# Recurrence operands parked in DRAM, a gate product of 256 columns, and the order of the branch products

## The chip, the cores and the metric

One Trainium2 chip, one of its cores. The kernel is one launch; the metric is the device time of that launch in microseconds. Engines are called by the profile's short names: PE (TensorE, matrix products into PSUM; PEld are its weight loads), DVE (VectorE), ACT (ScalarE), POOL (GpSimd) and SP (SyncE, which here only issues transfers between DRAM and the on-chip memory).

## The reference

Two layers of a hybrid backbone over 512 tokens (256 context, 256 latent) of width 1024. Each layer mixes tokens in two branches and then runs a mixture of 32 experts. What matters here is the mixing:

```
p = h @ w_in                                  # one projection, split by columns
y_rw  = rwkv7_branch(...)                     # 16 heads, recurrence in both directions
y_ssm = ssm_branch(...) * silu(z)             # 32 heads in 8 groups, both directions, gate z
merged = sigmoid(g_rw) * (y_rw @ w_branch_rw) + sigmoid(g_ssm) * (y_ssm @ w_branch_ssm)
out = merged @ w_out
# the recurrence, per head, per token:
sa = S @ a_t
S  = S * w_t + sa b_t^T + v_t k_t^T
y_t = S @ r_t
```

The second layer needs outputs for the latent tokens only, so its branch products, gates and outputs run over 256 tokens instead of 512; its recurrences still pass over all 512.

## The kernel before, in words

Every call of an engine goes through a recorder (`Recorder`, L246 and on), which keeps all calls of a layer, their dependences and their tiles. `finish` gives each call a latest start (`lst`) from the due time of its stream (`rec.at(phase, stream, goal)`), and `schedule` then lists the calls engine by engine: at each step the call that can start first by a table of costs, and among calls that could start at once the one with the earliest `lst`. A tile's slot is part of that: `SLOTS` says how many tiles of a name may live at once, `CLASS` how many slots of a size there are, and a call whose tiles have no slot waits. The emitted order is fixed, and each engine, SP's queue too, takes its instructions in that order. All instructions therefore have one line, L682.

A layer's mixing has three kinds of stream (`mix_streams`): eight pairs of recurrence heads (`rw`), eight state-space groups (`ssm`) with their branch gates (`gate`), and in layer 0 the modulation of the later stages. For a pair, `rw_prep` projects r, k and v (weights come in as `wst`, are split into `wh` and `wl`), and `rw_dir` builds for each direction the products of the chunked recurrence: `Z` (two operands side by side), `XT`, and by `psg` the triangular matrices `QA` and `AR`; `SU` holds the values v by chunk. `rw_solve` inverts the unit triangular matrices on DVE, row by row: `slB` and `slW` are its strip transposes in, 31 pairs of a product `slM` and a reduction into `slY`, and `slO` the transpose out; `rw_merge` (`psW`, `psZ`) completes `TT`. `rw_chain` then forms, per direction, `psat` and `psav`, from them with `TT` `psta` and `psua`, then `psgt` (into `GT`), `psH` and `psra`, and runs the seven steps of state `St` over the chunks, `psH` and `psY`. `rw_out` normalizes (`gy<-psm`), multiplies by the gate (`psgate`) and writes the pair's result to `rwd` in DRAM (`rwo`, `rwq`).

The names r, k, v, Z, XT, AR, QA, SU, TT have as many slots as one pair needs (one, or two for the two directions); `St` uses the slot of `rw_dir`'s `X`, and `GT` that of the solve's `slW`.

`ssm_group` convolves x, B and C on DVE (`cva`), and per 128 tokens computes the gate z: 2 halves of 8 x 3 products of 128 columns (`psz`). Results go to `smd` in DRAM, gates to `gd`.

`merge` loads `rwd` (`rwt`), `smd` (`smt`) and `gd` (`mg`), and for each of eight column blocks j forms the branch products (`psbr`), 24 for R (recurrence) and 48 for S and T (state space), then the gated sum `mhl`; after that the output product `pso`. `route` and `expert`/`expert_rows` follow.

Of the kernel before, what the change touches and what calls it, by code (L numbers as in the profile page):

```python
# [12 lines left out]
F32 = mybir.dt.float32  # L13
# [8 lines left out]
NT = 512  # L22
# [64 lines left out]
def _mix_pieces():  # L87
# [8 lines left out]
    for i in range(8):  # L96
        for n, o in (("x", X_ + 256 * i), ("y", X_ + 256 * i + 128), ("B", B_ + 128 * i), ("C", CC_ + 128 * i),
                     ("z", Z_ + 256 * i), ("u", Z_ + 256 * i + 128)):
            p.append((f"{n}{i}", "in", r(o, 128)))
    for j in range(8):  # L100
        p += [(f"R{j}", "rw", r(128 * j, 128)), (f"S{j}", "ssm0", r(128 * j, 128)), (f"T{j}", "ssm1", r(128 * j, 128))]
# [5 lines left out]
_KDIM = {"in": 8, "rw": 8, "ssm0": 8, "ssm1": 8, "out0": 4, "out1": 4}  # L107
# [20 lines left out]
def pack(i):  # L128
# [7 lines left out]
    src = {"in": f["w_in"], "rw": f["w_branch_rw"], "ssm0": f["w_branch_ssm"][:, :1024],  # L136
# [72 lines left out]
SLOTS = {"R": 2, "sp": 2, "t5": 4, "y5": 3, "rt5": 5, "ot": 2, "z1": 4, "wst": 2, "wh": 2, "wl": 2, "rwst": 1, "rwh": 1, "rwl": 1, "r": 1,  # L209
# [3 lines left out]
CLASS = {"c4": 18, "c2": 40, "c1": 23, "ps": 8}  # L213
# [8 lines left out]
ENGINES = tuple(LAT)  # L222

# [34 lines left out]
class _Pool:  # L258
# [3 lines left out]
    def tile(self, shape, dtype, name=None, tag=None, bufs=None):  # L262
# [6 lines left out]
        if ph == 1:  # L269
            if self.psum and tag == "g":  # L270
                tag = "t"
            if tag in SPLIT and self.rec.stream[0] in ("rw", "sh"):
                tag = "r" + tag
        else:
            tag = f"{tag}.{ph}"
# [410 lines left out]
class Kernel:  # L686
# [10 lines left out]
    def setup(self):  # L697
# [8 lines left out]
        self.unit = t("unit", [128, 512], BF16)  # L706
        self.tri = t("tri", [128, 256], F16)
        self.io = t("io", [128, 256])
        self.iota, self.low = self.io[:, 0:128], self.io[:, 128:256]
# [10 lines left out]
        self.rwd = self.dram.tile([128, 8, 2, NT], F16, name="rwd")  # L720
        self.smd = self.dram.tile([128, 16, 2, NT], F16, name="smd")
# [3 lines left out]
    def constants(self):  # L725
# [4 lines left out]
        u = t([128, 512], F32, "unit32")  # L730
        nc.sync.dma_start(u, i["unit"].rearrange("p j t -> p (j t)"))
        nc.vector.tensor_copy(self.unit, u)
        nc.sync.dma_start(self.io, i["cst"][:, C_WS:C_T64F])
# [322 lines left out]
    def rw_prep(self, l, i):  # L1056
# [23 lines left out]
        vp = rp.tile([128, 64 + NT + 64], F32, name="v", bufs=2)  # L1080
        G.memset(vp[:, 0:64], 0.0)
        G.memset(vp[:, 64 + NT:], 0.0)
        v = S["v"] = vp[:, 64:64 + NT]
# [26 lines left out]
        for w0_ in (0, 4, 8):  # L1110
            pv = self.psum("t", [128, 4, 128], "psv")
            n = min(4, 9 - w0_)
            for w in range(n):
                T.transpose(pv[:, w], vp[:, 64 * (w0_ + w):64 * (w0_ + w) + 128], self.ident)
            if w0_ < 8:
                A.activation(SU[0][64:128, w0_:w0_ + 4, 0], pv[64:128, :, 0:64], AF.Copy)
            a = 0 if w0_ else 1
            A.activation(SU[0][0:64, w0_ + a - 1:w0_ + n - 1, 1], pv[0:64, a:n, 64:128], AF.Copy)
# [118 lines left out]

    def rw_solve(self, i):
# [16 lines left out]
        G.tensor_copy(Y.rearrange("p j t -> p (j t)"), self.unit)  # L1255
# [62 lines left out]
    def rw_chain(self, l, i):  # L1318
# [18 lines left out]
        def batch(name, cs, out, lhs, rhs):  # L1337

            ps = out or self.psum("g", [128, 8, 64], name)
            with nc.together():  # L1340
                for c in cs:
                    for e in E:
                        T.matmul(ps[rows[e], c], lhs(c, e), rhs(c, e), start=True, stop=True)
            return ps

        for d in range(2):
            SU = S["SU"][d]
            TT, XT, Z, AR = [S[x, d] for x in ("TT", "XT", "Z", "AR")]
            qa = S["QA", d].rearrange("p (c e) t -> p c e t", e=2)
            all8 = range(8)  # L1350
            mid = seq[d][1:7]

            ps = batch("psat", all8, None, lambda c, e: Z[rows[e], c, 0], lambda c, e: self.ident[rows[e], 64 * e:64 * e + 64])
            at = wk.tile([128, 8, 64], F32, name="at", tag="slY")
            A.activation(at, ps, AF.Copy)
            ps = batch("psav", all8, None, lambda c, e: qa[rows[1 - e], c, e], lambda c, e: SU[rows[1 - e], c, e])
            av = wk.tile([128, 8, 64], F32, name="av", tag="slB")
            V.tensor_copy(av, ps)
# [4 lines left out]
            ps = batch("psua", all8, None, lambda c, e: TT[rows[e], c], lambda c, e: av[rows[e], c])  # L1363
            A.activation(SU[rows[0], :, 0], ps[rows[0]], AF.Copy)
            V.tensor_copy(SU[rows[1], :, 1], ps[rows[1]])
            ps = batch("psgt", mid, None, lambda c, e: qa[rows[e], c, e], lambda c, e: XT[rows[e], c, 64 * e:64 * e + 64])
# [816 lines left out]
```

## Time and profile before

| | |
|---|---|
| time, median of 3 runs | 3539.37 us (3537.98 to 3549.52) |
| the profiled execution: its time, its span | 3538.96 us, 3537.1 us |
| PE, PEld busy | 3110.2 us (88%), 2094.7 us (59%) |
| DVE busy | 2447.3 us (69%) |
| ACT, POOL busy | 1705.4 us (48%), 769.3 us (22%) |
| bytes moved by DMA | 662.65 MB, 187 GB/s on average |
| granted PE clock, mean | 0.940 of full speed |

Busy times are averages over stages with different limits, so the rows below cut the span: layer 0's mixing until about 1350, its experts until about 2000, layer 1's mixing until about 2990, its experts to the end. In the view by windows a row reads: from:to in us, the length, then busy time (with the count of instructions) of PE, PEld, DVE, ACT and POOL, the mean granted PE clock, the mean busy share of the 16 DMA engines, and GB/s. The clock has two levels, 1.2 and 2.4 GHz; a mean between 0.5 and 1 tells how much of the stretch was at either. In a timeline or a chain of waits a row begins with its start and its length in us; "[... <-X]" is idle time before it and who ended it.

### The profile page before, as it was taken

What the parts mean: (1) busy time and instruction counts of PE and PEld (TensorE: products, weight loads), DVE (VectorE), ACT (ScalarE), POOL (GpSimd) and SP (SyncE); (2) the same over time, 40 slices, a digit from 0 to 9 for tenths busy, and PEclk for the clock granted to TensorE, in tenths of its full rate; (3) what the DMA queues carried; (4) which work ended last, traced back from release to release, by engine and by line L of the source; (5) the groups of instructions that cost most, each with busy time, mean ns of one, the idle gap of its engine ahead of it and who ended that gap; (6) DMA issues with size and microseconds to landing.
All of it is one profiled execution on the core that took longest, in us unless ns stands there. A gap on an engine that the chain in (4) does not pass through costs nothing. (4 is left out here: it accounts for less than half of the span.)

```text
span 3537.1 us, 86322 instructions
## 1 busy us (share of the span) xinstructions
PE 3110.2 (88%) x36050; PEld 2094.7 (59%) x36050; DVE 2447.3 (69%) x4491; ACT 1705.4 (48%) x3155; POOL 769.3 (22%) x1080
## 2 busy tenths in 40 slices
PE   7899889898998998999998778888889789899987
PEld 3566466475566457888886455666566668333332
DVE  4868868768778337999997788788988765221112
ACT  4554454454544325998886645554545434111111
POOL 1332332333232111111111133232333311000000
PEclk9999999999999997999999899999999889899998
DMA  7032231421312736999996411221212138999996
GB/s 283 28 106 73 93 118 51 151 100 43 120 57 98 276 104 222 412 401 397 396 394 249 154 63 45 74 69 50 75 61 71 53 125 299 346 399 398 399 398 243
DMA packets 241746, 662.65 MB, mean 187 GB/s; under 512 B 26688, under 2 KB 55104, under 8 KB 241344
## 3 DMA queue, kind: packets, MB, share of 16 engines
q1 hardware_dynamic: 236608, 640.22, 49.1%
q10 hardware_dynamic: 3584, 12.58, 0.9%
q8 instruction: 287, 4.70, 0.5%
q0 software_dynamic: 1152, 4.19, 0.3%
q14 instruction: 115, 0.94, 0.1%
HBM read 622.30 MB, written 34.60 MB: 186 GB/s over the span
## 5 line engine op out<-in xcount | busy, mean ns | idle before, releaser
L682 PE MATMUL mm<-h,wh 128*128 128x512 f16 (+1 forms) x2432 | 680.4, 363 | 11.0 <-ACT wh L682 11.0
L682 PEld LDWEIGHTS <-wh 128*128 128x128 f16 x3200 | 311.4, 99 | 280.7 <-issue 25.4
L682 PE MATMUL mm<-h,wl 128*128 128x512 f16 (+2 forms) x1216 | 439.0, 362 | 39.2 <-DVE wl L682 39.1
L682 DVE SCALAR_TENSOR_TENSOR ewl<-est,ewh 128x1024 f16<-128x1024 f32 x352 | 411.7, 1222 | 15.5 <-ACT ewh L682 12.4
L682 ACT ACTIVATE ewh<-est 128x1024 f16<-128x1024 f32 x384 | 382.6, 1049 | 32.4 <-PE pse L682 28.3
L682 DVE SCALAR_TENSOR_TENSOR wl<-wst,wh 128x1024 f16<-128x1024 f32 (+1 forms) x234 | 293.2, 1267 | 35.0 <-ACT wh L682 34.5
L682 PE MATMUL pse<-xg,ewh 128*128 128x96 f16 x4096 | 276.5, 206 | 2.9 <-DVE xg L682 0.8
L682 PEld LDWEIGHTS <-ewh 128*128 128x128 f16 x4096 | 265.8, 98 | 7.1
L682 PEld LDWEIGHTS <-wl 128*128 128x128 f16 (+1 forms) x1600 | 159.4, 100 | 181.4 <-DVE wl L682 47.9
L682 PE MATMUL pse<-xg,ewl 128*128 128x96 f16 x2048 | 264.0, 206 | 0.3 <-issue 0.2
L682 ACT ACTIVATE wh<-wst 128x1024 f16<-128x1024 f32 (+1 forms) x234 | 240.2, 1043 | 12.2 <-DMA wst<-in_wmix_dram 11.6
L682 PE MATMUL pse<-esh,xg 128*64 128x512 f32 x512 | 236.3, 597 | 0.0
L682 PE MATMUL pse<-est,xg 128*64 128x512 f32 x512 | 236.3, 597 | 0.0
L682 DVE SCALAR_TENSOR_TENSOR cva<-cvz,cwh,cva 128x512 f32<-128x512 f32 (+1 forms) x256 | 204.0, 797 | 0.4
L682 PEld LDWEIGHTS <-ewl 128*128 128x128 f16 x2048 | 199.4, 98 | 5.8 <-issue 4.1
L682 DVE TENSOR_TENSOR slM<-slY,slW 128x144 f32<-128x144 f32 (+22 forms) x496 | 175.0, 353 | 6.4
L682 POOL TENSOR_TENSOR ewl<-est,ewh 128x1024 f16<-128x1024 f32 x32 | 69.7, 2180 | 487.5 <-ACT ewh L682 414.6
L682 DVE SCALAR_TENSOR_TENSOR eyl<-psy,egs,eyh 128x512 f16<-128x512 f32 x32 | 24.0, 751 | 211.2 <-ACT eyh L682 211.2
L682 PEld LDWEIGHTS <-h 128*128 128x128 f16 x2496 | 150.0, 102 | 27.0 <-issue 21.1
L682 POOL TENSOR_TENSOR sht<-shz 128x512 f32<-128x512 f32 (+3 forms) x56 | 65.2, 1164 | 403.7 <-ACT shz L682 244.4
L682 PE MATMUL psz<-wh,h 128*128 128x128 f16 x1536 | 149.4, 225 | 0.0
L682 PE MATMUL psz<-wl,h 128*128 128x128 f16 x768 | 139.9, 225 | 8.3 <-DVE wl L682 8.3
(561 smaller groups left out, 7072.7 us busy)
## 6 DMA issues: line engine op xcount, KB each, us to landing
est<-in_w_dram SPq DMA_DIRECT2D x576, 512.0 KB, 7.5
wst<-in_wmix_dram SPq DMA_DIRECT2D x246, 512.0 KB, 4.7
esh<-in_w_dram SPq DMA_DIRECT2D x384, 256.0 KB, 6.6
wst<-in_wmod_dram SPq DMA_DIRECT2D x96, 512.0 KB, 6.0
ys<-ey ACTq DMA_DIRECT2D x32, 384.0 KB, 6.9
lot<-in_lora_dram SPq DMA_DIRECT2D x16, 256.0 KB, 4.8
gd<-gat SPq DMA_DIRECT2D x16, 256.0 KB, 2.0
smd<-smo SPq DMA_DIRECT2D x16, 256.0 KB, 3.4
```

The source lines that it names most:

```text
L682: r = getattr(e, m)(*[real(x) for x in a], **{n: real(x) for n, x in k.items()})
```

## The change

Three things change.

1. *Parked operands.* `psat` and `psav` move from `rw_chain` to the end of `rw_dir`, with their results in place of the operands that they used up (`Z[:, :, 0]`, the free halves of `SU`). `rw_dir` then stores Z, SU, XT and AR to DRAM (`sd`), `rw_prep` stores bv (`sbv`); `rw_chain` and `rw_out` load them back into new tiles of the same names. The chain's due time is one pair later (`LAG = 1`, stream `ch`), so that its calls stand behind the next pair's products. `GT` has a slot of its own; `St` keeps that of `X`.
2. *The gate z.* Its weights are cut by rows of w_in (512 and 512) instead of by columns (128 and 128), so that a token tile takes 2 x 4 x 3 products of 256 columns.
3. *Branch products.* In `merge` all S and T products with their gates come first (`gated(1, j)`, due from `t0` on), then the loads of `rwt`, then the R products.

Beside this v has no zero pads (two of its transposes become products with the identity), the solve's start value is set by a memset and a copy of 2 columns, and a constant of the router is loaded when it is needed.

```
@@ _KDIM
-_KDIM = {"in": 8, "rw": 8, "ssm0": 8, "ssm1": 8, "out0": 4, "out1": 4}
+_KDIM = {"in": 8, "in0": 4, "in1": 4, "rw": 8, "ssm0": 8, "ssm1": 8, "out0": 4, "out1": 4}
...
-SLOTS = {"R": 2, "sp": 2, "t5": 4, ...
+SLOTS = {"GT": 1, "t5": 4, ...
-CLASS = {"c4": 18, "c2": 40, "c1": 23, "ps": 8}
+CLASS = {"c4": 18, "c2": 41, "c1": 23, "ps": 8}
+LAG = 1
...
@@ rw_prep
+        nc.sync.dma_start(self.sb_[:, i, :NT - o0], bv[:, :NT - o0])
@@ rw_dir, at its end
+        ps = self.batch("psat", lambda c, e: Z[rows[e], c, 0], lambda c, e: self.ident[rows[e], 64 * e:64 * e + 64])
+        A.activation(Z[:, :, 0], ps, AF.Copy)
+        ps = self.batch("psav", lambda c, e: QA[rows[1 - e], 2 * c + e], lambda c, e: SU[rows[1 - e], c, e])
+        A.activation(SU[rows[0], :, 0], ps[rows[0]], AF.Copy)
+        V.tensor_copy(SU[rows[1], :, 1], ps[rows[1]])
+        sd = self.sd[:, i, d]
+        nc.sync.dma_start(sd[:, 0], Z.rearrange("p c b t -> p (c b t)"))
+        nc.sync.dma_start(sd[:, 1], SU.rearrange("p c b t -> p (c b t)"))
+        nc.sync.dma_start(sd[:, 2], XT.rearrange("p c t -> p (c t)"))
...
@@ rw_chain
-        GT = wk.tile([128, 2, 8, 64], F32, name="GT", tag="slW")
+        GT = wk.tile([128, 2, 8, 64], F32, name="GT")
...
+            Z = S["Z", d] = rp.tile([128, 8, 2, 64], F32, name="Z", bufs=4)
+            nc.sync.dma_start(Z.rearrange("p c b t -> p (c b t)"), sd[:, 0])
...
-            ps = batch("psta", all8, None, lambda c, e: TT[rows[e], c], lambda c, e: at[rows[e], c])
-            A.activation(qa[rows[0], :, 0], ps[rows[0]], AF.Copy)
-            V.tensor_copy(qa[rows[1], :, 1], ps[rows[1]])
+            ps = batch("psta", lambda c, e: TT[rows[e], c], lambda c, e: Z[rows[e], c, 0])
+            A.activation(Z[:, :, 0], ps, AF.Copy)
...
@@ ssm_group
-                self.proj_t(pz[:, 128 * b:128 * b + 128], self.h, slice(128 * t, 128 * t + 128), Wz[b], 0, 128)
+                self.proj_t(pz, lambda k: self.h(4 * b + k), tk, Wz[b], 0, 256, first=b == 0, last=b == 1)
@@ merge
+        sgs = []
+        for j in range(8):
+            nc.at(2, ("bs", j), self.t0 + (j + 1) * step * 0.67)
+            sgs.append(gated(1, j))
+        nc.at(2, ("br", 0), self.t0 + 8 * step * 0.67)
...
+            nc.at(2, ("br", j), self.t0 + step * (5.36 + (j + 1) * 0.33))
+            sg = [gated(0, j), sgs[j]]
@@ mix_streams
+            rec.at(1, ("ch", i), h + 60e3 + P * (i + 1 + LAG) + 1e3)
             rec.tight = True
             self.rw_chain(l, i)
```

What this does to the order is seen at three places. First, DVE in a layer-1 period. Before, a solve ends (`slO`) and the chain's rows (`av`, `QA`, `SU`, `GT`) come behind it:

```order
L682 TENSOR_REDUCE slY<-slM 128x8
L682 TENSOR_TENSOR yg<-yg,zt 128x256
L682 STREAM_TRANSPOSE slO<-slY 128x32x16
L682 TENSOR_TENSOR yg<-yg,zt 128x256
L682 STREAM_TRANSPOSE TN<-slO 32x256 x2
L682 STREAM_TRANSPOSE TT<-slO 32x8x32 x4
L682 SCALAR_TENSOR_TENSOR v<-shz,mu_30552,sht 128x512
L682 SCALAR_TENSOR_TENSOR wl<-wst,wh 128x1024
L682 COPY av<-psav 128x512
L682 TENSOR_SCALAR yss<-yss 128x2
L682 TENSOR_TENSOR E<-E 128x512
L682 SCALAR_TENSOR_TENSOR wl<-wst,wh 128x1024
```

After, the chain's rows stand between the rows of the next pair's solve:

```order
L683 TENSOR_TENSOR slM<-slY,slW 128x196
L683 SCALAR_TENSOR_TENSOR cva<-cvz,cwh,cva 128x512
L683 TENSOR_TENSOR GT<-psgt,id_65 128x192
L683 TENSOR_REDUCE slY<-slM 128x2x7
L683 TENSOR_TENSOR GT<-psgt,id_65 128x192
L683 TENSOR_TENSOR slM<-slY,slW 128x256
L683 TENSOR_TENSOR Z<-Z,psra 128x4x64
L683 TENSOR_REDUCE slY<-slM 128x2x8
L683 TENSOR_SCALAR St<-psH,pl 128x64
L683 TENSOR_TENSOR slM<-slY,slW 128x128
```

The chain's `GT`, `Z` and `St` have moved from behind one solve into the next one.

Second, SP's queue in a layer-1 period. Before, weight loads stand there, with the few transfers of a pair between them:

```order
L682 DMA rwd<-rwq 128x2x256
L682 DMA log<-in_lora_dram 128x256
L682 DMA wst<-in_wmix_dram 128x1024
L682 DMA lot<-in_lora_dram 128x512
L682 DMA wst<-in_wmix_dram 128x1024 x6
L682 DMA gd<-gat 128x256
L682 DMA wst<-in_wmix_dram 128x1024 x2
L682 DMA smd<-smo 128x2x256 x2
L682 DMA gd<-gat 128x256
```

After, a direction's stores, each with a reload behind it (of the pair before, into the slot that the store frees), stand between two weight loads:

```order
L683 DMA wst<-in_wmix_dram 128x1024
L683 DMA sd<-XT 128x1024
L683 DMA XT<-sd 128x1024
L683 DMA sd<-AR 128x512
L683 DMA AR<-sd 128x512
L683 DMA sd<-Z 128x1024
L683 DMA Z<-sd 128x1024
L683 DMA sd<-SU 128x1024
L683 DMA SU<-sd 128x1024
L683 DMA sd<-XT 128x1024
L683 DMA XT<-sd 128x1024
L683 DMA wst<-in_wmix_dram 128x1024
```

Eight stores and eight reloads a pair (and one of each for bv) have come into the queue.

Third, PE at the end of layer 1's mixing, where the last chain ends (`psY`, `psm`) and the branch products (`psbr<-smt` for S and T) begin. Before:

```order
L682 MATMUL psY<-Z,St 64x64 x16
L682 MATMUL psrow<-cst,mc_70 128x128 x4
L682 MATMUL psm<-gy,cst 128x256
L682 MATMUL psst<-cst,sq 128x2 x2
L682 LDWEIGHTS wh
L682 MATMUL psbr<-smt,wh 128x256
```

After:

```order
L683 MATMUL psm<-gy,cst 128x256
L683 MATMUL psst<-cst,sq 128x2 x2
L683 MATMUL psspread<-cst,sprd 128x128 x2
L683 LDWEIGHTS gw
L683 MATMUL psgate<-sg,gw 128x256
L683 LDWEIGHTS gw
L683 MATMUL psgate<-sg,gw 128x256
L683 LDWEIGHTS gw
L683 MATMUL psgate<-sg,gw 128x256
L683 LDWEIGHTS gw
L683 MATMUL psgate<-sg_30516,gw 128x256
L683 LDWEIGHTS wh
L683 MATMUL psbr<-smt,wh 128x256
```

The first S product stood ahead of the last pair's `psspread` and `psgate`, with R products (`psbr<-rwt`) among those of S; now it stands behind `psgate`, and the R products stand behind all of S and T.

## Rows read from the trace of the kernel before

**Rows 1.** busy time of PE, PEld, DVE, ACT, POOL, then clock, DMA, by stage
```profile
141.40:1074.50 933.10, 843.54 (x10326) 568.67 (x10325) 718.38 (x1473) 450.11 (x1007) 298.97 (x429) 0.96 0.27 93
...
1074.50:1195.80 121.30, 106.83 (x1309) 71.73 (x1308) 77.59 (x170) 43.49 (x91) 20.58 (x32) 0.93 0.48 172
...
1195.80:1350.00 154.20, 153.96 (x918) 89.90 (x917) 63.91 (x70) 46.78 (x57) 23.50 (x18) 1.00 0.40 137
...
2067.70:2821.50 753.80, 640.11 (x8137) 473.46 (x8136) 630.92 (x1336) 378.87 (x830) 251.62 (x412) 0.93 0.20 63
...
2821.50:2899.20 77.70, 61.26 (x902) 48.21 (x900) 61.44 (x145) 27.51 (x59) 13.57 (x25) 0.85 0.25 81
...
2899.20:2990.80 91.60, 85.07 (x756) 74.60 (x757) 48.20 (x62) 35.05 (x44) 13.48 (x14) 0.98 0.82 280
...
2990.80:3537.10 546.30, 476.28 (x3242) 187.47 (x3240) 119.34 (x292) 83.08 (x148) 6.04 (x5) 0.91 0.95 364
```

**Rows 2.** DVE timeline: first and last slW of both layers (start us, us)
```profile
141.40 1.97 DVE L682 STREAM_TRANSPOSE slW<-slB 128x1024 f32<-128x1024 f32 x1
...
1074.50 1.95 DVE L682 STREAM_TRANSPOSE slW<-slB 128x1024 f32<-128x1024 f32 x1
...
2067.71 1.98 DVE L682 STREAM_TRANSPOSE slW<-slB 128x1024 f32<-128x1024 f32 x1
...
2821.55 1.93 DVE L682 STREAM_TRANSPOSE slW<-slB 128x1024 f32<-128x1024 f32 x1
```

**Rows 3.** the same windows view, one layer-1 period in three parts
```profile
2503.20:2555.00 51.80, 42.87 (x315) 29.95 (x313) 49.20 (x117) 23.48 (x48) 18.16 (x30) 0.90 0.16 45
2555.00:2582.60 27.60, 27.07 (x688) 22.62 (x687) 19.12 (x40) 16.95 (x42) 5.19 (x8) 1.00 0.28 90
2582.60:2608.10 25.50, 21.09 (x169) 14.74 (x167) 22.11 (x38) 14.85 (x30) 13.31 (x23) 0.93 0.28 88
```

**Rows 4.** DVE timeline: where those parts begin and end
```profile
2503.18 1.95 DVE L682 STREAM_TRANSPOSE slW<-slB 128x1024 f32<-128x1024 f32 x1
...
2555.05 1.07 DVE L682 STREAM_TRANSPOSE slO<-slY 128x512 f32<-128x512 f32 x1
...
2582.64 0.42 DVE L682 SCALAR_TENSOR_TENSOR gy<-psm,gy 128x256 f32<-128x256 f32 x1 [3.10 <-PE psm L682]
...
2608.12 1.94 DVE L682 STREAM_TRANSPOSE slW<-slB 128x1024 f32<-128x1024 f32 x1
```

**Rows 5.** chain of waits, layer-1 tail (start us, us, what)
```profile
2908.82 5.87 DMA rwd<-rwq
...
2914.71 2.17 DMA rwt<-rwd
...
2916.92 46.93 PE psbr L682 x413
```

**Rows 6.** groups by line, seven layer-1 periods (count, busy us, mean ns)
```profile
L682 DVE COPY QA<-psta 64x512 f32<-64x512 f32 x14 | 9.7, 695 | 3.3 <-PE psta L682 1.5 <-ACT QA L682 1.4
...
L682 ACT ACTIVATE SU<-psua 64x512 f32<-64x512 f32 x14 | 8.3, 590 | 11.5 <-DVE SU L682 11.5
```

**Rows 7.** timeline of SP's queue at the layer-1 tail
```profile
2889.41 1.64 SPq L682 DMA_DIRECT2D wst<-in_wmix_dram  x3
```

**Rows 8.** DMA issues (count, KB each, median us to landing)
```profile
wst<-in_wmix_dram SPq DMA_DIRECT2D x246, 512.0 KB, 4.7
...
xd<-xres SPq DMA_DIRECT2D x6, 512.0 KB, 3.0
```

**Rows 9.** what SP's queue waited for, seven layer-1 periods
```profile
SPq L682 <- DVE wl L682: 234.0, 19, 28.5
```

**Rows 10.** chain of waits: a gate tile at either clock
```profile
2211.70 2.68 PE psz L682 x48
...
2318.63 5.17 PE psz L682 x47
```

**Rows 11.** windows view: ten us of 256-column branch products
```profile
2930.00:2940.00 10.00, 10.00 (x94) 8.95 (x93) 5.50 (x7) 3.26 (x4) 0.72 (x1) 1.00 0.83 295
```

More of the change, by code (lines that the diff above doesn't have):

```diff
@@ L271, in tile @@
                 tag = "t"
[L272 removed]
+            if tag in SPLIT and self.rec.stream[0] in ("rw", "sh", "ch"):
                 tag = "r" + tag
@@ L1109, in rw_prep @@
         S["SU"] = SU
-        for w0_ in (0, 4, 8):
+        for w0_ in (0, 4):
             pv = self.psum("t", [128, 4, 128], "psv")
[L1112 to L1116, printed above, removed]
+            with nc.together():
+                for w in range(4):
+                    if w + w0_:
+                        T.transpose(pv[:, w], v[:, 64 * (w0_ + w) - 64:64 * (w0_ + w) + 64], self.ident)
+            if not w0_:
+                with nc.together():
+                    T.matmul(pv[64:128, 0], v[:, 0:64], self.ident, start=True, stop=True)
+                    T.matmul(pv[0:64, 0], v[:, NT - 64:NT], self.ident, start=True, stop=True)
+                A.activation(SU[0][0:64, 7, 1], pv[0:64, 0, 64:128], AF.Copy)
+            A.activation(SU[0][64:128, w0_:w0_ + 4, 0], pv[64:128, :, 0:64], AF.Copy)
             a = 0 if w0_ else 1
-            A.activation(SU[0][0:64, w0_ + a - 1:w0_ + n - 1, 1], pv[0:64, a:n, 64:128], AF.Copy)
+            A.activation(SU[0][0:64, w0_ + a - 1:w0_ + 3, 1], pv[0:64, a:4, 64:128], AF.Copy)
         G.tensor_copy(SU[1][64:128, :, 0], SU[0][64:128, :, 0])
@@ L1236, in rw_dir, with batch @@
                                     mi[:, None, :].to_broadcast([128, 4, 64]), op=OP.mult)
+        rows = self.rows2
+        SU = S["SU"][d]
+        ps = self.batch("psat", lambda c, e: Z[rows[e], c, 0], lambda c, e: self.ident[rows[e], 64 * e:64 * e + 64])
[7 more added lines that the diff above has]
+        nc.sync.dma_start(sd[:, 2], XT.rearrange("p c t -> p (c t)"))
+        if full:
+            nc.sync.dma_start(sd[:, 3], AR.rearrange("p c t -> p (c t)"))
+        else:
+            nc.sync.dma_start(sd[:, 3, 512:], AR[:, 8:].rearrange("p c t -> p (c t)"))
+    rows2 = (slice(0, 64), slice(64, 128))
+    def batch(self, name, lhs, rhs, cs=range(8)):
+        ps = self.psum("g", [128, 8, 64], name)
+        with self.nc.together():
+            for c in cs:
+                for e in range(2):
+                    self.nc.tensor.matmul(ps[self.rows2[e], c], lhs(c, e), rhs(c, e), start=True, stop=True)
+        return ps
     def rw_solve(self, i):
@@ L1346, in rw_chain @@
-        for d in range(2):
[L1347 to L1350, printed above, removed]
-            mid = seq[d][1:7]
[L1353 to L1358, printed above, removed]
-            ps = batch("psta", all8, None, lambda c, e: TT[rows[e], c], lambda c, e: at[rows[e], c])
-            A.activation(qa[rows[0], :, 0], ps[rows[0]], AF.Copy)
-            V.tensor_copy(qa[rows[1], :, 1], ps[rows[1]])
-            ps = batch("psua", all8, None, lambda c, e: TT[rows[e], c], lambda c, e: av[rows[e], c])
+        batch = self.batch
@@ L1603, in merge, with gated @@
         ts = slice(o0, NT)
-        nc.at(2, ("br", 0), self.t0)
+        step = 15e3 if full else 8e3
+        nc.at(2, ("bs", 0), self.t0)
+        sm = [self.tile([128, 2, NT], F16, "smt", bufs=16) for _ in range(16)]
+        for j in range(16):
+            nc.sync.dma_start(sm[j][:, :, ts], self.smd[:, j, :, ts])
+        xs0, xs1 = lambda k: sm[k], lambda k: sm[8 + k]
+        def gated(b, j):
+            t = self.tile([128, NT], F32, f"mg{b}", bufs=8 if b else 2)[:, :n]
+            nc.sync.dma_start(t, self.gd[:, 8 * b + j, ts])
+            ps = self.psum("g", [128, NT], "psbr")[:, :n]
+            if b == 0:
+                self.proj(ps, self.load(l, f"R{j}"), 0, 128, xrw, ts)
+            else:
+                self.proj(ps, self.load(l, f"S{j}"), 0, 128, xs0, ts, last=False)
+                self.proj(ps, self.load(l, f"T{j}"), 0, 128, xs1, ts, first=False)
+            V.scalar_tensor_tensor(t, t, 1.0, ps, op0=OP.add, op1=OP.mult)
+            return t
+        sgs = []
[3 more added lines that the diff above has]
+        nc.at(2, ("br", 0), self.t0 + 8 * step * 0.67)
         rw = [self.tile([128, 2, 2, NT], F16, "rwt", bufs=4) for _ in range(4)]
@@ L1790, in route @@
             for u in range(t + 1):
-                T.matmul(pp[:, t], self.low if u == t else self.c(C_ONE), at[:, u], start=u == 0, stop=u == t)
+                T.matmul(pp[:, t], low if u == t else self.c(C_ONE), at[:, u], start=u == 0, stop=u == t)
         pos = tl("pos")
```

77 lines of the change are left out of this document (32 added, 45 removed).

## The prediction

> **What bounds the kernel now.** I read the stages first [rows 1]. The two mixing stages are where the change works: in layer 0 seven pair periods lie between 141.4 and 1074.5, in layer 1 seven between 2067.7 and 2821.5. Each period runs from one solve (the strip transpose that writes slW) to the next; the first and last of them in both layers stand in [rows 2], so a period is 933.1 / 7 = 133.3 us in layer 0 and 753.8 / 7 = 107.7 us in layer 1. Per period TensorE is busy 843.5 / 7 = 120.5 us and VectorE 718.4 / 7 = 102.6 us in layer 0; 640.1 / 7 = 91.4 us and 630.9 / 7 = 90.1 us in layer 1. No engine fills a layer-1 period, so something serial does.
>
> Then one layer-1 period cut at its own rows [rows 3, 4]. The solve takes from 2503.2 to 2555.0: VectorE is busy 49.2 of 51.8 us, TensorE 42.9, at a granted clock of 0.90. Then the chain, until gy at 2582.6: TensorE 27.1 of 27.6, VectorE only 19.1. Then the next pair's products up to the next slW: VectorE 22.1 of 25.5. The three follow each other, because the next pair's Z, SU, XT, AR and QA have two slots each, which the chain holds to its end, and St and GT sit in the slots of X and slW. So VectorE loses about 14 us of 107.7 where TensorE is full, and TensorE loses about 9 us in the solve, some of it at the lower clock. In layer 0 TensorE is the fuller engine (90%).
>
> After the mixing, TensorE leaves 6.5 of 91.6 us open in layer 1's tail and 14.5 of 121.3 in layer 0's [rows 1]; the rest of layer 0's branch products run solid. The layer-1 opening is the wait for the last pair: rwd lands, rwt lands, and only then the long run of psbr [rows 5].
>
> **The change, part by part.**
>
> *Parked operands and the lag.* After the change the chain of pair i no longer stands between solve i and the products of pair i+1; it reloads its operands into the slots that pair i+1 has just stored from, and its rows stand inside solve i+1 (first place in the order). What is left in series is solve plus products, 51.8 + 25.5 = 77 us with the small merge behind the solve, below what VectorE has to do in a period; so VectorE's own work becomes the bound in layer 1 and TensorE's in layer 0. VectorE loses the half copy into QA twice a pair (0.695 us each [rows 6]) and gains a memset of slY, which no row prices; it lies between 0 and that copy, and I take 0.2: 90.1 - 1.4 + 0.2 = 88.9 us. ScalarE gains two half copies of SU (0.59 us each [rows 6]), hidden: it is busy 379 of 753.8 us [rows 1]. The products psat and psav stay the same 64 matmuls a direction, only earlier. How full can VectorE get? In the solve it is 95% full, in the rest of the period 41.2 / 53.1 = 78%. With the chain's rows under the solve only the products stage still has holes; I take 90%, between 84% now and 95%: 88.9 / 0.90 = 99 us. Bounds: 93.6 at 95%, 106 at today's 84%. Seven periods: 7 x (107.7 - 99) = 61 us (12 to 99). In layer 0 I take TensorE at 95% of a period: 120.5 / 0.95 = 127 us, bounds 119 (full, and the part of it that ran at 1.2 GHz back at 2.4) and 133.3 (nothing). Seven periods: 44 us (0 to 100). The stage from the last solve to the end of the last chain (77.7 us in layer 1) has no further solve to hide in and stays.
>
> *The transfers.* A layer-1 pair adds 8 stores, 8 reloads and 2 for bv, 7.6 MB; now a period moves 63 GB/s x 107.7 us = 6.8 MB. Together 14.4 MB in 99 us is 145 GB/s; layer 0 comes to about 21 MB in 127 us, 168 GB/s. The expert stage of layer 1 holds 364 GB/s at a share of 0.95 [rows 1], so width is there. The price is on SP's queue: 18 issues at 0.55 us [rows 7] are 10 us of queue in 99, and each reload waits until the store from its slot has landed, 3.0 us for 512 KB [rows 8]. Behind it stand the weight loads (second place in the order). What covers that is their slack: SP's queue today waits 234 us of the 753.8 for a weight buffer to come free [rows 9], so loads run as early as the buffers allow. I take 0, with the other end as the first rival.
>
> *Gate products at 256 columns.* 48 matmuls of 128 columns become 24 of 256. A gate tile at the full clock takes 2.68 us, 56 ns each; at the lower clock 5.17 us for 47, 110 ns [rows 10]. 256-column products run 94 in 10 us, 106 ns [rows 11]. So 24 of them take 2.55 us: 0.13 us a tile, 48 tiles in both layers, 6 us at the most, of which the part in layer 1 lies beside VectorE. I count it inside the periods, as 0.
>
> The Trainium skill, "TensorE: Matmul & The Clock Gate", section "Back-to-back issue gap", says that a stream of weight load and matmul pairs is paced by both, about 81 ns a pair at 128 columns. By that a tile would cost 48 x 81 ns = 3.9 us and the edit would give some 1.3 us a tile, an estimate of 60 us over 48 tiles. The 56 ns of this trace do not agree with it.
>
> *State-space branch products first.* The work is the same 576 products a layer. In the new order the first of them stands behind the last psgate (third place), so what they can fill is the trip of the last rwq through DRAM: 5.87 + 2.17 us [rows 5], and the 6.5 us that TensorE leaves open there. I take 6 us in layer 1 and 5 of the 14.5 in layer 0, bounds 0 and 20 together. The expert weights stand behind the last branch weights in SP's queue as before, so that stage, which is at the transfer limit (0.95), moves with its start, one for one.
>
> *The small edits* (v without its pads, unit as two columns, low loaded late) touch GpSimd, busy a third of a period at most: 0, hidden by that.
>
> Sum: the profiled execution took 3538.96 us, 1.9 over its span and 0.4 under the median of the runs. 3539.0 - 61 - 44 - 11 = **3423 us**. Its own range, from half the gain to a third more of it: 3380 to 3475.
>
> **Rivals.**
>
> *SP's queue becomes the bound* (slower). A direction's cluster of four stores and four reloads takes 4 x 3.0 + 8 x 0.55 = 16 us, in which the weight loads behind it do not start, and they land 4.7 us after their issue [rows 8]. Three staged weights of 24 products, each 2.6 us at 256 columns and 5.1 at 512, cover some 9 us. Then TensorE stands 7 us twice a period: 99 + 14 = 113 and 127 + 14 = 141, which is 7 x 5.3 + 7 x 7.7 - 11 = +80: 3619 us. It decides once a cluster is 4 us longer than the cover in layer 1. For it: today's 11 weights a layer-1 period have three buffers only, and the queue serves in order. Against: the 234 us of slack. Chance 0.14.
>
> The Trainium skill, "DMA: Bandwidth & Descriptors", section "Rules for kernel authors", speaks for this rival: a transfer that reads what another wrote has to wait for the other's completion, and one queue does not order them. No row of this trace shows a store and its reload back to back.
>
> *The chain stretches the solve.* Its 19.1 us of VectorE now compete with a solve in which VectorE has 2.6 us open; the solve gets longer by what the products stage loses: 104 and 131, -26 - 16 - 5: 3492 us. For it: 95% in the solve. Against: the new order moves convolution and weight-split rows out of it. Chance 0.20.
>
> *Everything fits.* 92 and 119 us, tails -20, and the clock at 1.00 (now 0.93 and 0.96): -110 - 100 - 20: 3309 us. Against: no 50 us of mixing runs so full today. Chance 0.10.
>
> *The gate edit pays by itself*: were the pairs paced by their weight loads, 60 us more: 3363. The 56 ns speak against it. Chance 0.03.
>
> *The lag changes nothing*, because the periods are bound by work that is only moved: 3539. Against: VectorE and TensorE are both 15% open in layer 1. Chance 0.03.
>
> **How the numbers follow.** Forecast 0.50, rivals 0.14, 0.20, 0.10, 0.03, 0.03. Less than 0.3% (about 10 us, what this kernel can show) counts as no change. Faster: 0.50 + 0.20 + 0.10 + 0.03, less a hundredth for the edge: 0.82; slower 0.14; same 0.04. The range leaves out most of the slow rival and of the full fit, about 0.2: 3335 to 3540.
>
> **What would show it.** Right: slW to slW near 99 us in layer 1 and 127 in layer 0; GT between slM rows; VectorE above 88% of the seven layer-1 periods; the granted clock above 0.93. Wrong: TensorE waiting for wl whose wst landed late while SP waits for a landing of sd (the queue); a solve above 60 us with full VectorE (the stretch); periods as now. The forecast fails if the periods stay within 3 us of today's, or if the time comes from the gate tiles.

## The result and the profile after

The changed kernel takes 3494.81 us, median of 4 runs (3485.52 to 3500.19), against 3541.14 us for the kernel before on the same chip: a ratio of 0.986, 95% interval 0.9835 to 0.989. It is 46 us faster, where 116 were forecast. The profiled execution took 3495.24 us with a span of 3493.4, so the two profiles differ by 43.7 us. Of these TensorE's idle time (the span less its busy time) gave 60.4 (426.9 us before, 366.5 after), and its busy time took 16.7 back (3110.2 us before, 3126.9 after).

The same stages, cut at the changed kernel's own rows (windows view; from:to, length, busy time of PE, PEld, DVE, ACT, POOL, clock, DMA share, GB/s). They answer to [rows 1]:

```profile
151.70:1034.10 882.40, 814.49 (x9199) 530.57 (x9197) 696.12 (x1439) 446.55 (x1006) 285.40 (x405) 0.97 0.46 165
1034.10:1142.40 108.30, 98.95 (x1408) 69.19 (x1403) 75.28 (x173) 39.15 (x89) 21.71 (x32) 0.94 0.58 202
...
2040.60:2771.60 731.00, 634.10 (x7473) 459.31 (x7473) 605.78 (x1307) 375.45 (x821) 246.73 (x389) 0.92 0.40 134
2771.60:2851.30 79.70, 69.94 (x1086) 55.65 (x1084) 62.95 (x158) 32.29 (x73) 16.68 (x30) 0.91 0.53 176
2851.30:2945.00 93.70, 86.77 (x743) 73.50 (x744) 51.92 (x64) 38.85 (x47) 16.28 (x14) 0.95 0.82 287
2945.00:3493.40 548.40, 479.98 (x3255) 189.32 (x3253) 119.39 (x292) 82.97 (x148) 6.04 (x5) 0.91 0.95 363
```

The cuts are the first and last slW of each layer (DVE timeline), which answer to [rows 2]:

```profile
151.67 1.92 DVE L683 STREAM_TRANSPOSE slW<-slB 128x1024 f32<-128x1024 f32 x1
...
1034.11 1.94 DVE L683 STREAM_TRANSPOSE slW<-slB 128x1024 f32<-128x1024 f32 x1
...
2040.65 1.96 DVE L683 STREAM_TRANSPOSE slW<-slB 128x1024 f32<-128x1024 f32 x1
...
2771.57 1.89 DVE L683 STREAM_TRANSPOSE slW<-slB 128x1024 f32<-128x1024 f32 x1
```

Seven periods now take 882.4 us in layer 0 (933.1 before) and 730.9 in layer 1 (753.8). A layer's last chain ends where the last `gy<-psm` stands on DVE: in layer 0 before, in layer 0 after, in layer 1 after (in layer 1 before it is the cut at 2899.2 of [rows 1]).

```profile
1163.89 0.69 DVE L682 SCALAR_TENSOR_TENSOR gy<-psm,gy 128x512 f32<-128x512 f32 x1 [3.23 <-PE psm L682]
...
1142.42 0.69 DVE L683 SCALAR_TENSOR_TENSOR gy<-psm,gy 128x512 f32<-128x512 f32 x1 [4.09 <-PE psm L683]
...
2851.32 0.42 DVE L683 SCALAR_TENSOR_TENSOR gy<-psm,gy 128x256 f32<-128x256 f32 x1 [2.69 <-PE psm L683]
```

Piece by piece, beside the forecast:

| piece | forecast | measured |
|---|---|---|
| start to first solve, layer 0 | 0 | +10.3 (151.7, was 141.4) |
| seven layer-0 periods | -44 | -50.7 |
| last layer-0 solve to its last chain's end | 0 | +18.9 (108.3, was 89.4) |
| from there to layer 1's first solve | -5 | -5.6 (898.2, was 903.8) |
| seven layer-1 periods | -61 | -22.9 |
| last layer-1 solve to its last chain's end | 0 | +2.1 (79.8, was 77.7) |
| from there to the end | -6 | +4.2 (642.1, was 637.8) |

A mean hides how layer 1's gain is spread. Its second solve starts here, before and after:

```profile
2173.38 1.94 DVE L682 STREAM_TRANSPOSE slW<-slB 128x1024 f32<-128x1024 f32 x1
...
2128.54 1.93 DVE L683 STREAM_TRANSPOSE slW<-slB 128x1024 f32<-128x1024 f32 x1
```

The first period, which with the lag holds only the head of a chain (28 of the 104 `psH`), takes 87.9 us (105.7 before); the other six take 643.0 together, 648.2 before. So of the 22.9 us the first period gives 17.8, and the later periods are hardly shorter than they were.

A late layer-1 period in two parts, solve and rest, to be read beside [rows 3], and a late layer-0 period (windows view):

```profile
2553.00:2593.50 40.50, 35.78 (x424) 23.34 (x422) 37.70 (x100) 19.51 (x41) 10.11 (x17) 0.96 0.24 86
2593.50:2665.10 71.60, 61.52 (x703) 47.33 (x704) 51.12 (x94) 36.32 (x81) 26.28 (x41) 0.88 0.46 153
632.50:767.40 134.90, 125.65 (x1430) 80.83 (x1428) 105.17 (x214) 69.68 (x153) 44.23 (x58) 0.97 0.47 167
```

The second direction's chain lies under the solve, and the solve became shorter, 40.5 us for 51.8. At the end of this period the first direction's `psta`, `psua`, `psgt` and `psra` and a part of its `psH` and `psY` do not: they stand ahead of the next solve, among the products. The rest, forecast at the products' 25.5 us plus what fits in, takes 71.6, and VectorE is busy in 71% of it. Over the seven periods VectorE is at 605.78 / 731 = 83%, about as before (84%), not at 90%.

What stops the rest is seen in TensorE's timeline (start, length, idle time before and who ended it):

```profile
2648.66 0.38 PE L683 MATMUL mm<-h,wh 128*128 128x256 f16 x2
2653.17 1.97 PE L683 MATMUL psta<-Z,TT 64*64 64x64 f32 x32 [4.12 <-DMA Z<-sd]
2655.07 1.97 PE L683 MATMUL psx<-cst,X 128*128 128x128 f32 x8
...
2661.26 1.16 PE L683 MATMUL psg<-Z,X 64*128 64x128 f32 x16
```

`psta`, the first product of the parked chain, stands ahead of `psx` and `psg` of the next pair's second direction. It waits for its reload, which stands in SP's queue right behind the store of the next pair's Z (timeline of SP's queue, then the store's row of the DMA issues):

```profile
2646.17 0.37 SPq L683 DMA_DIRECT2D sd<-Z  x1
2646.59 0.42 SPq L683 DMA_DIRECT2D Z<-sd  x1
...
sd<-Z SPq DMA_DIRECT2D x32, 512.0 KB, 4.7
```

The reload goes out 0.42 us behind the store, so it does not wait until the store has landed, for which the median is 4.7 us. What it waits for is its turn: the queue keeps its order, and the store ahead of it goes out only when its operand is complete (ScalarE ends `Z<-psat` at 2645.7). From the reload's issue to `psta` pass 6.6 us; the next solve cannot start until the `psg` behind it is done. After the wait TensorE runs at a mean granted clock of 0.70 for ten us, so part of that stretch is at 1.2 GHz:

```profile
2653.10:2663.00 9.90, 9.83 (x155) 8.48 (x157) 3.60 (x8) 2.90 (x5) 0.00 (x0) 0.70 0.61 190
```

Over layer 1's seven periods such waits are the largest and a smaller one of TensorE (waits view: total, times, longest):

```profile
PE psta L683 <- DMA Z<-sd: 18.5, 7, 4.1
...
PE psua L683 <- DMA SU<-sd: 5.8, 4, 2.0
```

The Trainium skill, "DMA: Bandwidth & Descriptors", section "Rules for kernel authors", says that a read of what another transfer wrote has to wait for that transfer's completion. These two rows do not show that case: the reload reads what the pair before had stored a period earlier. The cost did not come by weight loads late behind the cluster, where I had put it, but at the engine that uses the reloaded data.

### The profile page after: what moved, and what is told of

It reads as the page before. It is cut to its first block, busy times and chain, and to the rows that moved or that the text cites. A ratio compares the mean times of both kernels' runs of the same rounds, so it can differ in the third digit from the quotient of the medians.

```text
span 3493.4 us, 84573 instructions
## 1 busy us (share of the span) xinstructions
PE 3126.9 (90%) x34930; PEld 2073.5 (59%) x34930; DVE 2422.0 (69%) x4474; ACT 1725.8 (49%) x3189; POOL 771.4 (22%) x1048
## 5 line engine op out<-in xcount | busy, mean ns | idle before, releaser
L683 ACT ACTIVATE ewh<-est 128x1024 f16<-128x1024 f32 x384 | 380.4, 1049 | 13.7 <-PE pse L683 10.3
L683 DVE SCALAR_TENSOR_TENSOR wl<-wst,wh 128x1024 f16<-128x1024 f32 (+1 forms) x234 | 293.5, 1262 | 42.7 <-ACT wh L683 41.6
L683 ACT ACTIVATE wh<-wst 128x1024 f16<-128x1024 f32 (+1 forms) x234 | 241.7, 1042 | 52.8 <-DMA wst<-in_wmix_dram 51.8
L683 DVE TENSOR_TENSOR slM<-slY,slW 128x144 f32<-128x144 f32 (+22 forms) x496 | 162.7, 328 | 8.3
L683 ACT ACTIVATE eu<-pse 128x384 f32<-128x384 f32 (+1 forms) x64 | 34.4, 538 | 243.9 <-PE pse L683 240.0
L683 DVE TENSOR_REDUCE slY<-slM 128x2 f32<-128x4 f32 (+23 forms) x496 | 147.3, 297 | 7.2
L683 PE MATMUL psz<-wh,h 128*128 128x256 f16 x768 | 150.0, 282 | 0.0
```

The source lines that it names most:

```text
L683: r = getattr(e, m)(*[real(x) for x in a], **{n: real(x) for n, x in k.items()})
```

## The experiments

All are timed against the kernel before on the same chip (medians of 3540.13 to 3543.71 us). First four, to split the change and to price the trip through DRAM.

**e1_gate**: the kernel before with the gate edit alone.

```
-  self.proj_t(pz[:, 128*b:128*b+128], self.h, ..., Wz[b], 0, 128)
+  self.proj_t(pz, lambda k: self.h(4*b + k), ..., Wz[b], 0, 256, first=b == 0, last=b == 1)
```

> The kernel before with the gate z at 256 columns and nothing else. Theory (a pair of 128 columns costs 56 ns, one of 256 columns 106 ns): 0.13 us a tile, at most 6 us in all, so 3535 to 3541 us. Rival (the gate edit carries the gain of the change): 3495 us, and shorter periods in the later part of each layer too.

3502.74 us, ratio 0.9884 (0.9859 to 0.9909): 41 us faster. My theory missed, and the rival seemed to hold. But its products cannot give that much, and TensorE's waits changed in rows that the edit does not touch. The waits view of the kernel before, then of this one, with the first row of its page:

```profile
PE psx L682 <- POOL X L682: 49.4, 11, 6.7
PE psBT L682 <- DVE Bc L682: 43.0, 11, 6.1
PE mm L682 <- DVE wl L682: 39.1, 17, 7.9
```

```profile
PE mm L682 <- DVE wl L682: 55.5, 18, 8.2
...
PE psx L682 <- POOL X L682: 20.7, 5, 6.6
...
PE psBT L682 <- DVE Bc L682: 16.5, 9, 6.0
...
PE 3084.2 (88%) x34898; PEld 2046.7 (58%) x34898; DVE 2432.5 (69%) x4491; ACT 1700.2 (49%) x3155; POOL 775.0 (22%) x1080
```

Two waits for late operands of GpSimd and VectorE fall by 55 us together, but others rise, that of `mm` for wl by 16. Of the 36.3 us between the two profiles TensorE's idle time gave only 10.3 (426.9 to 416.6); its busy time gave 26.0 (3110.2 to 3084.2), at a mean granted clock of 0.949 in place of 0.940.

**e5_gate_split** keeps the order of e1_gate and undoes the width.

```
+  if tile is psz: issue columns 0:128, then 128:256, in place of 0:256
```

> The kernel with the gate edit alone gained 41 us (3502.7 against 3543.7), far over the 6 us that its products can give. This one has the same order of work as that kernel on every engine, but each gate product is issued as two of 128 columns, as in the kernel before. Theory 1 (the gain is in the order that the planner made from slightly other prices): 3503 to 3512 us. Theory 2 (256 columns help by themselves, by fewer weight loads): 3535 to 3545 us.

3510.46 us, 0.9925 (0.9899 to 0.995). The first row of its page:

```profile
PE 3092.9 (88%) x36050; PEld 2074.4 (59%) x36050; DVE 2430.6 (69%) x4491; ACT 1702.0 (49%) x3155; POOL 773.4 (22%) x1080
```

So of the 41 us some 33 are the order that the planner made from slightly other prices, and 7.7 the width: 0.16 us a tile over 48 tiles, where 0.13 was forecast. The two intervals meet, but TensorE's busy time says about the same, 8.7 us. In the profiles the order gave 28.0 us, and 17.3 of them are busy time of TensorE with as many products as before (36050), at a mean granted clock of 0.948 for 0.940. So more than half of what the order gave is the clock that the same products got. That also answers the rule of the Trainium skill ("TensorE: Matmul & The Clock Gate", "Back-to-back issue gap"), by which the estimate was 60 us: the runs do not agree with it.

**e6_no_gate**: the changed kernel without the gate edit (the lines of e1_gate turned round).

> The changed kernel without the gate edit: parked operands, lag and the order of the branch products stay. Theory 1 (the gate edit's gain adds to the rest): 3530 to 3540 us, so that parking, lag and branch order together give about 5 us. Theory 2 (with the lag the gate edit's order gives nothing): 3490 to 3500 us.

3498.35 us, 0.9876 (0.9849 to 0.9903), 3.5 us over the changed kernel. Theory 2 holds: the gate edit's order and the lag's do not add up. The gate edit alone gives 41 of the 46 us, parking, lag and branch order without it 45. Beside e1_gate TensorE's idle time in the changed kernel falls by 50.1 us, but its busy time rises by 42.7, at a mean granted clock of 0.941 for 0.949. Layer 0 ends its last chain at 1166.4 us here, at 1163.9 in the kernel before: up to there parking with the lag gave layer 0 nothing by this pair. At layer 1's first solve it is 4.0 us ahead.

**e7_before_drain** and **e8_after_drain** move a number of the planner that has nothing to do with the change, to see how far orders of equal work scatter.

```
-DRAIN = 105
+DRAIN = 100
```

> The kernel before with one number of the planner moved (DRAIN 100 instead of 105 ns, its price for a change of TensorE's tile mode); the work is the same, only its order differs. If orders of equal work scatter little: 3535 to 3550 us. If they scatter as the gate edit's 41 us suggest: anywhere from 3500 to 3560 us.

> The changed kernel with the same number of the planner moved (DRAIN 100 instead of 105 ns). If orders of equal work scatter little: 3485 to 3500 us. If they scatter by the gate edit's size: 3460 to 3530 us, and then the 20 us that the later chain gained is no proof of its cause by itself.

3536.29 us (0.9986, 0.9971 to 1.0001) against 3542.99, and 3510.2 us (0.9923, 0.99 to 0.9946) against the changed kernel's 3494.8: 7 us one way, 15 the other (21 by the two ratios). With the 33 us of e5, a difference of that size between kernels whose orders differ proves no cause. Only e3 and e5 hold the order, and e9 up to the merges.

**e2_lag0**: parking without lag.

```
-LAG = 1
+LAG = 0
```

> The changed kernel with LAG = 0: operands are stored and loaded back, but a chain is due in its own period again. Theory (the gain of the periods comes from the lag; parking alone gives nothing): layer-1 periods of 107 us and layer-0 periods of 133 us as in the kernel before, 3525 to 3545 us. Rival (what helps is that parking frees the slots early, or the order of the branch products): 3495 us with LAG = 0 too.

3541.0 us, 0.9987 (0.9974 to 1.0001). As the theory said in the whole, though not in its parts: layer 0's periods sum to 956.5 us, layer 1's to 742.1. The page's first row:

```profile
PE 3141.8 (89%) x34930; PEld 2089.8 (59%) x34930; DVE 2408.9 (68%) x4474; ACT 1728.0 (49%) x3189; POOL 769.4 (22%) x1048
```

Beside e1_gate parking without lag (and the branch order) costs 38 us, which the lag pays back. No TensorE wait for sd is among them. In the profiles 35 of them lie in layer 0 up to its last chain (1174.8 us for 1140.0); TensorE's idle time is 18.9 us less than in e1_gate and its busy time 57.6 more, at a mean granted clock of 0.933 for 0.949. Why the clock is lower there no run showed. Beside the changed kernel, where LAG alone differs, the lag is worth 46 us, 32 of them in layer 0 up to its last chain; the orders differ, too.

**e3_other_data**: the changed kernel, order kept on TensorE, VectorE and ScalarE, without the stores. The reloads stay, read other data, and no longer stand behind a store.

```
   for m, a, k in o.calls:
+      if m == "dma_start" and a[0] is sd: continue          # no store
+      a = [w1[0, pair, direction] if x is sd else x for x in a]   # reload: other data
```

> The changed kernel with the same order on TensorE, VectorE and ScalarE, but without the 112 stores of Z, SU, XT and AR; the reloads read as many bytes from expert weights, so the chains work on other numbers. Theory (the trip through DRAM lies on the path of a steady period, because psta stands in TensorE's order ahead of the next direction's products): no wait of psta and psua for sd (24 us in layer 1 and 9 us in layer 0 now), periods shorter by 2 to 4 us, 3440 to 3465 us. Rival 1 (the periods are bound by the work of TensorE and VectorE, and the trip is only where a hole happens to lie): the waits go, others of the same size take their place, 3485 to 3500 us. Rival 2 (the queue of SP holds up weight loads): a gain as in the theory, but in waits for wst and wl.

3468.16 us, 0.9788 (0.9763 to 0.9813): 27 us under the changed kernel, 3 us short of the theory's range. The place shown above, in this kernel:

```profile
2631.65 1.13 PE L687 MATMUL psg<-Z,X 64*128 64x128 f32 x14 [0.27 <-DVE X L687]
...
2633.25 1.15 PE L687 MATMUL psta<-Z,TT 64*64 64x64 f32 x32
2634.33 1.09 PE L687 MATMUL psx<-cst,X 128*128 128x128 f32 x8
...
2638.68 1.16 PE L687 MATMUL psg<-Z,X 64*128 64x128 f32 x16
```

No wait: with no store ahead of it the reload of Z went out 12.9 us before its `psta`, in place of 6.6, although a reload takes about as long as before (median from issue to landing 6.0 us, 6.4 in the changed kernel).

```profile
2620.32 0.42 SPq L687 DMA_DIRECT2D Z<-in_w_dram  x1
```

The products run faster, too: `psta` and `psx` take 1.15 and 1.09 us in place of 1.97: the ten us around them run at full clock, though the eleven before them do not.

```profile
2620.00:2631.00 11.00, 9.77 (x126) 8.79 (x125) 6.31 (x12) 7.61 (x17) 8.55 (x16) 0.69 0.75 245
2631.00:2641.00 10.00, 9.73 (x195) 8.09 (x197) 9.81 (x19) 2.91 (x5) 0.00 (x0) 1.00 0.34 114
```

Layer 1's seven periods fall from 730.9 to 704.8 us (100.7 each, the forecast had 99); layer 0's stay, 883.5 for 882.4. First and last solve of layer 1 here:

```profile
2039.08 1.97 DVE L687 STREAM_TRANSPOSE slW<-slB 128x1024 f32<-128x1024 f32 x1
...
2743.84 1.89 DVE L687 STREAM_TRANSPOSE slW<-slB 128x1024 f32<-128x1024 f32 x1
```

The 24.3 us of waits for sd are gone, and 26.2 are gained, though not wait by wait: the last four periods, where all of `psta`'s waits lie, give 24.8 us, the first three 1.4. In layer 0 some 9 us of such waits go, and nothing is gained. TensorE works 93% of a late period there (125.65 of 134.9 us above); that it has other products in those places is my reading, not shown. Weight loads gained nothing that TensorE waits for (waits view of the changed kernel, then of this one), which excludes a queue that holds up the weights:

```profile
PE mm L683 <- DVE wl L683: 3.6, 5, 1.3
...
PE mm L687 <- DVE wl L687: 5.0, 6, 1.4
```

**e4_late_chain**: the trip stays, the chain stands later.

```
+  if m == "dma_start" and the source is sd: o.lat += 10000   # ns, in the planner
```

> The changed kernel with the planner told that a reload of sd takes 10 us longer; nothing else. In the order it makes, psta of the first direction stands behind psx, psg and psat of the second direction in most periods. Theory (trip through DRAM in front of the next direction's products): the 4 us wait before psta is filled, steady layer-1 periods 112 to about 107, 3450 to 3475 us. Rival 1 (work bound): 3485 to 3500 us. A chain that starts later can also end behind the next solve, which would cost: 3500 to 3530 us.

3476.09 us, 0.9813 (0.9787 to 0.9839), 19 us under the changed kernel, 1 us over the forecast's range. By e8 that alone would prove nothing. But no wait for sd is left on TensorE, and layer 1's periods sum to 707.6 us, 23 less than in the changed kernel, where e3 gave 26; layer 0's sum to 890.1, 8 more. A long wait of TensorE that stays is that for X of GpSimd, 25.7 us in all.

**e9_old_merge**: the changed kernel with R, S and T products by column block again; the order ahead of the merges is the same.

```
-  sgs: gated(1, j) for all j; then rwt; then gated(0, j)
+  rwt; then for each j: gated R, gated S and T
```

> The changed kernel with the branch products in the order of the kernel before (R, S and T by column block); the order ahead of the two merges is the same. Theory 1 (the new order fills the trip of the last pair's result, as forecast): 11 us more, 3500 to 3512 us. Theory 2 (TensorE has other products there anyway): within 4 us of the changed kernel, 3488 to 3500 us.

3485.29 us, 0.9847 (0.9825 to 0.9869): 9.5 us less without the edit, below both theories, with intervals that overlap. In the changed kernel the first S product waits behind the last pair's normalization (TensorE timeline of the changed kernel, then of this one):

```profile
2852.24 0.61 PE L683 MATMUL psst<-cst,sq 128*128 128x2 f32 x4 [0.96 <-ACT sq L683]
2854.64 0.69 PE L683 MATMUL psspread<-cst,sprd 128*128 128x128 f32 x2 [1.79 <-ACT sprd L683]
2855.12 1.06 PE L683 MATMUL psgate<-sg,gw 128*128 128x256 f16 x4
2857.49 0.61 PE L683 MATMUL psbr<-smt,wh 128*128 128x256 f16 x2 [1.31 <-ACT wh L683]
2858.75 0.40 PE L683 MATMUL psbr<-smt,wl 128*128 128x256 f16 x1 [0.65 <-DVE wl L683]
```

```profile
2853.94 0.38 PE L683 MATMUL psspread<-cst,sprd 128*128 128x128 f32 x2
...
2855.68 0.60 PE L683 MATMUL psgate<-sg,gw 128*128 128x256 f16 x4
2860.31 0.48 PE L683 MATMUL psbr<-smt,wh 128*128 128x256 f16 x2 [4.02 <-DMA smt<-smd]
```

Four waits of 4.7 us together stand in place of one of 4.0 (and one of 1.2 two us later), so in waits nothing is gained. The stage from layer 1's last chain to the end is 642.1 us with the edit and 633.3 without; that from layer 0's last chain to layer 1's first solve 898.2 and 889.2.

**e10_l1_only**: e4_late_chain with lag and parking in layer 1 alone.

```
-  rec.at(1, ("ch", i), h + 60e3 + P * (i + 1 + LAG) + 1e3)
+  rec.at(1, ("ch", i), h + 60e3 + P * (i + 1 + l * LAG) + 1e3 * l)
+  if full: no stores, no reloads; the chain reads S["Z", d], S["SU"][d], ...
```

> Lag, parking and the later chain of e4_late_chain in layer 1 alone; in layer 0 the chain follows its own solve and reads its operands on the chip (psat and psav stay at the end of the products). Theory 1 (TensorE is full in layer 0, so the lag gives nothing there, and what it takes out of the periods the tail gives back): layer 0 up to its last chain as in the kernel with the gate edit alone, 1140 us, the whole 3465 to 3485 us. Theory 2 (the lag gives layer 0 the forecast 44 us): layer 0 up to its last chain 1165 us or more, the whole 3495 to 3520 us.

3493.64 us, 0.9861 (0.9841 to 0.988), 17.5 us over e4_late_chain. Layer 0's last chain ends at 1156.6 us, between the two theories; with the lag (e4_late_chain) it ends at 1147.8. So parking with the lag is worth 9 us there by this pair of kernels and -2.5 by e6, within the scatter in either case, and not 44. The cut at the last chain hides a part: behind it, up to layer 1's first solve, TensorE has 835.4 us to work here and 818.4 in e4_late_chain, and at that solve the two are 19.6 us apart (2063.20 and 2043.65).

**e11_pool_late**: e4_late_chain with the planner's latency of GpSimd raised by 1 us.

```
-LAT = {..., "gpsimd": 75, ...}
+LAT = {..., "gpsimd": 1075, ...}
```

> The kernel of e4_late_chain with the planner told that a result of GpSimd reaches the others 1 us later, since psx waits 25.7 us and psg 8.5 us there for X of GpSimd. Theory 1 (TensorE's waits at the head of its order are what is left to gain): these waits fall below 12 us, 3445 to 3470 us. Theory 2 (a wait taken away at one row comes back at another): 3465 to 3490 us.

3471.73 us, 0.9815 (0.9795 to 0.9835), 4 us under e4_late_chain, where the two theories overlap by time; theory 2, since the wait stays:

```profile
PE psx L687 <- POOL X L687: 26.4, 8, 5.7
```

**e12_due**: the changed kernel with a pair's products due 28 us earlier.

```
-  rec.at(1, ("rw", i), h + 60e3 + P * (i + 1))
+  rec.at(1, ("rw", i), h + 60e3 + P * (i + 1) - 28e3)
```

> The changed kernel with a pair's products and solve due 28 us earlier (the length of a chain, which its due time held before the lag); chains and all else as they were. Theory 1 (the lag took urgency from the products): first solve at 140 us instead of 151.7, and 10 to 20 us less in all, 3475 to 3485 us. Theory 2 (the order's chance decides): 3480 to 3515 us, with the first solve where it was.

3504.86 us, 0.9899 (0.9881 to 0.9917), 10 us slower. The first solve does start 16 us earlier:

```profile
135.63 1.94 DVE L683 STREAM_TRANSPOSE slW<-slB 128x1024 f32<-128x1024 f32 x1
```

Of these 16 us 12.5 are lost again by layer 0's last chain (1138.9 us, 1142.4 in the changed kernel). So the late first solve is explained by the due time; that it was no loss by itself is likely, but the order changed everywhere.

**e13_old_merge_late** (e11_pool_late with the edit of e9_old_merge) and **e14_all** (e4_late_chain with the edits of e9_old_merge and e12_due):

> The kernel of e11_pool_late with the branch products in the order of the kernel before. Theory 1 (the new order of the branch products costs some 9 us, as e9_old_merge suggests): 3458 to 3466 us. Theory 2 (the 9 us are within what runs differ): 3468 to 3476 us.

> The kernel of e4_late_chain (3476.1 us) with the branch products in the order of the kernel before and the due time of e12_due. If both parts pay what they should (9 and 10 to 20 us): 3445 to 3460 us. If the branch order alone pays: 3463 to 3470 us. If neither: 3470 to 3485 us.

3469.8 us, 0.9788 (0.9769 to 0.9808), and 3473.99 us, 0.9807 (0.9789 to 0.9824). The old order of the branch products gives 1.9 us in the first, within what runs differ, so its size stays open; the new order gains nothing in any pair. In e14 neither part shows. In e11 and e13 layer 1's seven periods take 692.8 and 690.9 us, the 99 us a period that were forecast, with the trip through DRAM in place and no wait for it on TensorE. e13_old_merge_late is the fastest of the kernels that leave nothing out, 73.8 us under the kernel before and, by intervals that do not meet, under the changed one.

## Why the prediction was wrong

*Layer-1 periods, the step that failed.* For the transfers "I take 0", I wrote, and with it VectorE at 90%. I had priced the trip through DRAM (store and reload) by the weight loads that stand behind it in SP's queue, where it costs nothing. I had not looked at when a reload comes to its turn behind the stores, who uses it, and what stands behind that instruction on its engine: the chain's `psta` on TensorE, ahead of the second direction's products on which the next solve waits. e3 measures this term: 26 us over layer 1's seven periods, 0 over layer 0's. It is the larger part of the 38 that are missing there (61 forecast, 22.9 measured). The other 12 stay without the stores: VectorE is then at 86% (602.85 of 703.8 us), not at 90. That the mean of 100.7 us comes so near to the 99 is in part luck: a first period with only the head of a chain is in it (87.2 us), the six others take 102.9 each, and VectorE's work came to 86 us a period, not 88.9. So the mechanism was there, this term was missing, and the filling was put too high. It is also not true that each reload waits until its store has landed, nor that it goes into the slot that the store frees: in e3 the reload goes out at 2620.3, before `psat` (2627.4) reads the Z that would be stored.

*Layer-0 periods.* 126.1 us each, forecast 127, and yet worth little. A lag of one leaves out a chain in the first period and hands it to the stage behind the last solve; that stage "stays", I wrote, but two chains lie there now, and it took 18.9 us back, while the first solve came 10.3 later: 21.5 us are left at the last chain. Of TensorE's work from first solve to last chain nothing goes away (843.5 + 74.9 = 918.4 us before, 814.5 + 99.0 = 913.4 after). Against the 44 forecast, parking with the lag is worth between -2.5 and 9 us at the last chain (e6, e10) and between 4 and 20 at layer 1's first solve, all within what orders scatter; its size stays open. The sum should have been made over the whole stage, from the first solve to the last chain.

*Branch products.* 11 us forecast, none found: in layer 1 the wait that goes comes back ahead of the first S product.

*Gate products.* The term was about right (0.16 us a tile, 7.7 us), though the sum counts it as 0; the rival "pays by itself" is wrong in its mechanism. That the new prices make the planner lay out all other work anew had no place in my sum, and in the kernel before that was worth 33 us by itself.

*The rivals.* The stretched solve gave 3492 us, next to the measured time, by a mechanism that is not there, so that is luck: the solve became shorter. SP's queue as the bound of the weight loads is refuted (waits of `mm` for wl 39.1 us before, 3.6 after), although a reload's turn in that queue is what comes late, and although a weight load lands later than in [rows 8], 6.2 us for 4.7. The total came right in sign; the two layers' gains that add up to it, 21.5 us from the start to layer 0's last chain and 20.8 us from layer 1's first solve to its last chain, were not proven one by one, since they are of the size of the scatter. The gate edit alone gives 41 of the 46 us, so that how much of them parking and the lag gave stays open; shown is what the trip costs them in layer 1.

*Two slips.* Half of the forecast 116 us and a third more than it lead to 3481 and 3384 us, not 3475 and 3380. And of the 14 us that VectorE loses in the period of [rows 3] TensorE is full in 8.5 only, in the chain (27.6 less 19.1).

## What to carry to other kernels

When operands are parked in DRAM, price the trip at the instruction that uses the reload: what stands behind it in its engine's order, and what stands ahead of the reload in the queue that issues it (with no store ahead it went out 12.9 us before its use, in place of 6.6). Not every such wait costs: in layer 0 nothing was gained without it. A software pipeline moves work from the first round to the tail, so sum over the whole stage and not over periods, and look at a period in the middle by itself. Where a planner sets the order, any edit reshuffles all of it: keep the order and change one thing (e3, e5), and run a neutral change of the planner's numbers to see what differences mean anything.

## What the runs showed of the hardware

A wait of 4.1 us on TensorE was followed by ten us at a mean granted clock of 0.70, where the same products without the wait ran at 1.00: `psta` took 1.97 us in place of 1.15. From the start of `psta` to the end of the `psg` behind it lie 9.3 us with the wait ahead of them and 6.6 without, so the wait cost 4.1 + 2.7 = 6.8 us at that place. Not all of the 2.7 is a net loss: without the wait a stretch of low clock lies eleven us earlier (0.69, above), there behind waits of 2.3 and 1.2 us, and over the 23 us around that place the mean is 0.85 in both kernels (2642.0 to 2665.0 here, 2620.0 to 2643.2 without the wait). The clock is also where orders of equal work differ: 36050 products kept TensorE busy for 3110.2 us in the kernel before, at a mean granted clock of 0.940, and as many for 3092.9 in e5_gate_split, at 0.948. A store and reload of 512 KB one behind the other take some 7 us from the store's issue to the first use; the reloads of Z alone have a median of 6.4 us:

```profile
Z<-sd SPq DMA_DIRECT2D x32, 512.0 KB, 6.4
```
